# Decay rows of a bidirectional SSD scan: forward in the first 64 partitions, backward in the other 64

## The chip, the cores and the metric

One core of a Trainium2 chip. The metric is the device time of one execution in microseconds, the median of several runs. The core has a matrix engine (TensorE, PE in the profile), a vector engine (VectorE, DVE), an activation engine (ScalarE, ACT), a general engine (GpSimd, POOL) and a queue that issues the DMAs (SyncE, SP). SBUF is the on-chip memory of 128 partitions, PSUM the memory that TensorE writes.

## The reference

An inference step with two layers over 128 prompt tokens and 512 sample tokens of width 1024. Layer 0 is a Conformer convolution branch. Layer 1 is a bidirectional Mamba-2 (SSD) branch with 32 heads of 64 channels, 4 groups of 8 heads, a state of 128, and chunks of 128 tokens. All is in float32.

```
xbc = silu(depthwise_conv(xbc, w_conv, b_conv))          # 5 taps
dt_f = softplus(dtr_f + bias_f);  dt_b = softplus(dtr_b + bias_b)
# ssd_scan, once forward, once on the flipped sequence; per chunk and head:
a_cum = cumsum(dt * a_neg)
seg = a_cum[..., :, None] - a_cum[..., None, :]
decay_mat = exp(where(lower, seg, -inf))
cb = einsum('bclgn,bcsgn->bcgls', cc, bc)
y_diag = einsum('bcgrls,bcsgrp->bclgrp', cb[:, :, :, None] * decay_mat, xdt)
chunk_states = einsum('bcsgn,bcgrs,bcsgrp->bcgrpn', bc, exp(a_cum[..., -1:] - a_cum), xdt)
y_off = einsum('bclgn,bcgrpn,bcgrl->bclgrp', cc, prev_state, exp(a_cum))
...
y = y_f + flip(y_b) + d_skip * xs
y = rms_norm_per_group(y * silu(z)) * norm_g
return y @ w_out, final states
```

For a source token s and a destination l of one chunk, the forward scan contributes where s <= l and the backward scan where s >= l. The kernel holds both in one 128 x 128 matrix per head: forward decay on one side of the diagonal, backward decay on the other; the diagonal's second share is added by itself.

## The kernel before

Layer 0 fills the time up to about 590 us and isn't touched. Layer 1 (`lp` pools, from line 590 of the code on) works on 640 tokens, 128 features to a tile. A weight tile of 128 x 1024 is loaded, split into a high part (ACT, L789) and a low part (a subtraction on DVE or POOL, L793), and multiplied by the modulated input in three passes (L827): 48 matmuls of 384 or 256 columns for each of the x, B, C and z tiles. The x, B and C tiles are then convolved (one ACT and four DVE instructions, L867 and L869), transposed to tokens (L893), and used by the SSD groups. `o` items are the output projection of a finished group. The last group's output projection and the final norm end the program (L1329 and after).

Before any group can begin, `time_steps` computes the step sizes on DVE and ACT (a chain of some 30 instructions over 128 x 384), writes the cumulated rows to a DRAM tensor `acd` (rows 0 to 63 forward, 64 to 127 backward, 32 heads for either half of the chunks) and turns four results into columns by TensorE transposes (`turn_columns`, L1460 to L1465). `cols1` holds, for each chunk, per source token the column of `v` (number 0) and an exponential (number 1); `cols2` holds the two weights.

A decay matrix is made in halves of four heads (`decay_half`): `gf` (forward rows) and `gb` (backward rows), 128 x 512 each, come by DMA from `acd`, with each row repeated over all 128 partitions. POOL subtracts a column value from each (L983, once for `gf`, once for `gb`), DVE copies `gb` over `gf` where a mask says so (L984), ACT takes the exponential (L986). DVE then multiplies by the C-B products in PSUM (L1161), and TensorE multiplies with x (`py`, L1170). There are 4 groups, 5 chunks and 2 halves: 40 of them. `gf` has 4 buffers, `gb` 2.

Other POOL work: `xw` (L1034), the decay of the states (L1053), the skip term and the sum of the states' share (`y`, L1117 and L1108).

The order of layer 1's instructions on each engine is made when the program is built, by a small planner (`class Order`). Each piece of work is a generator that yields operations with an engine and an expected duration; the planner keeps one clock for each engine, and issues at each step the operation that can start first, ties broken by a priority from `PRIO`. `either` offers two engines, the second with a bias in us. Rings (`get`, `put`) model the buffers, keys (`post`, `key`) the dependences. `PLAN` is the written order of the projections: `x20` is the tile 0 of group 2, and so on. The engines then run their lists in this order and wait on semaphores.

Of the kernel before, what the change touches and what calls it, by code (L numbers as in the profile page):

```python
# [41 lines left out]
def trunk(ctx: ExitStack, tc: tile.TileContext, a: dict):  # L42
# [574 lines left out]
    if True:  # L617
# [15 lines left out]
        msk = lp.tile([P, P], I32, name="msk")  # L633
# [28 lines left out]
        PE, ACT, VE, PO, SP = range(5)  # L662

        class Order:
            def __init__(self):
                self.clock = [0.0] * 5
                self.table = None
                self.keys = {}
                self.rings = {}
                self.chains = []  # L670
                self.count = 0
# [47 lines left out]
            def run(self, until=None):  # L719
                while self.chains:  # L720
# [4 lines left out]
                    for ch in self.chains:  # L725
                        if ch[4][0] != "op":
                            continue
                        ways, bias = (*ch[4][1:], 0.0)[:2]
                        for n, (eng, dur, fn, table) in enumerate(ways):
                            wait = MARGIN[eng] if ch[5] != eng else 0.0  # L730
                            t = max(self.clock[eng], ch[1] + wait)
                            load = 1.28 if table and table != self.table else 0.0
                            key = (t + 0.4 * load if len(ways) == 1 else t + dur - ways[0][1] + bias * n, ch[2], ch[3])
                            if best is None or key < best[0]:
                                best = key, ch, eng, t + load, dur, fn, table
                    if best is None:
                        break
                    _, ch, eng, t, dur, fn, table = best
# [3 lines left out]
                    self.clock[eng] = t + dur  # L742
                    ch[1] = t + dur + LATE.get(eng, 0.0)
# [5 lines left out]
        PRIO = {"x_after": 2, "filler": 3, "decay_half": 3, "decay_state": 1, "chain0": 0, "chain1": 0, "other_y": -3, "copy_y": -1, "split_y": -1, "groups": 0, "decays": -1, "norms": -3, "gate": 3, "products1": 3, "products0": 2, "residual0": 1, "final0": -2, "w_chain": 0, "time_steps": 1, "columns": 0, "logarithm": 0, "rows_out": 0, "ends_out": 1, "weights_out": 0, "first_steps": 0, "b_after": -2, "c_after": 0, "z_after": 2, "split": 3, "add_residual": 2, "out_weights": 1, "free_bc": -1, "final1": 3, "prompt": -3, "residual1": 0, "store": -1}  # L749
# [17 lines left out]
        for name, n in (("wf", 2), ("wh", 3), ("wl", 3), ("up", 0), ("xs", 3), ("bc", 2), ("Bt", 1), ("xt", 2), ("zs", 1), ("st", 6), ("xw", 2), ("gf", 4), ("gb", 2), ("y", 1), ("y3", 0), ("yo", 2), ("yhl", 0), ("tr", 1), ("b", 3)):  # L767
            run.ring(name, n)
# [11 lines left out]
        def w_load(i, src):  # L780
# [14 lines left out]
            def split():  # L795
# [3 lines left out]
                t = yield either((VE, 1.25, lambda: low(V)), (PO, 2.45, lambda: low(G)))  # L799
# [58 lines left out]
        def convolve(ps, j, tag, bufs, name, cell, u=None):  # L858
# [9 lines left out]
            for d in range(1, 5):  # L868
                t = yield op(VE, 0.95, lambda: V.scalar_tensor_tensor(out=acc, in0=u[:, d : d + PW], scalar=c("w_c", j * 5 + d), in1=acc, op0=ALU.mult, op1=ALU.add))  # L869
# [108 lines left out]
        def decay_half(g, n, hq, gf, gb, t0):  # L978
            ch, o8 = ORDER[g][n], 8 * g
            gfh, gbh = (z_.rearrange("p (h n) -> p h n", h=4) for z_ in (gf, gb))  # L980
            for back, gt in enumerate((gfh, gbh)):
                o = 32 * back + o8 + 4 * hq
                yield op(PO, 1.15, lambda: G.tensor_sub(out=gt, in0=gt, in1=cols1[ch][:, o : o + 4].unsqueeze(2).broadcast_to([P, 4, 128])))  # L983
            t = yield op(VE, 1.1, lambda: V.copy_predicated(out=gfh, mask=msk.unsqueeze(1).broadcast_to([P, 4, 128]), data=gbh))  # L984
            put("gb", t)
            t = yield op(ACT, 0.63, lambda: S.activation(out=gfh, in_=gfh, func=AF.Exp), "exp")  # L986
            grp[g][n, hq] = gfh
            post(("gf", g, n, hq), t)

        def decays():  # L990
            yield key(("cols",))
            for g in range(NG):
                for n, ch in enumerate(ORDER[g]):
                    for hq in range(2):
                        tiles = []
                        for back, (nm, bufs) in enumerate((("gf", 4), ("gb", 2))):
                            yield get(nm)

                            def load():
                                gt = lp.tile([P, 512], F32, tag=nm, bufs=bufs, name=nm)  # L1000
                                r, col = at(back, ch, 8 * g + 4 * hq)
                                nc.sync.dma_start(out=gt.rearrange("p (h n) -> p h n", h=4), in_=acd[r : r + 4, col : col + 128].unsqueeze(0).broadcast_to([P, 4, 128]))
                                tiles.append(gt)
                            t = yield op(SP, 0.1, load)
                        start(decay_half(g, n, hq, *tiles, t), t)

        def group(g):
# [23 lines left out]
            def chunk_state(ch, back, cell, *need):  # L1031
                yield get("xw")
                xw = lp.tile([P, 512], F32, tag="xw", bufs=2, name="xw")
                t = yield op(PO, 1.12, lambda: G.tensor_mul(out=D8(xw), in0=D8(xt[ch]), in1=bc64(cols2[ch], 32 * back + o8)))  # L1034
# [9 lines left out]
            def decay_state(step, back):  # L1044
# [8 lines left out]
                t = yield op(PO, 1.15, lambda: G.tensor_mul(out=D8(new), in0=D8(sts[back, ch]), in1=dec))  # L1053
# [3 lines left out]
            def chain(back):  # L1057
                for step in range(3):
# [8 lines left out]
                    t = yield op(VE, 0.62, lambda: V.tensor_add(out=new, in0=new, in1=cell[0]))  # L1067
# [26 lines left out]
            def states_y(ch, y, n):  # L1094

                l0 = cofs(ch)
                for back in range(2):
# [8 lines left out]
                    t = yield op(VE, 0.64, lambda: V.tensor_mul(out=D8(yo), in0=D8(po), in1=bc64(cols1[ch], (64, 96)[back] + o8)))  # L1106
                    put("b", t)
                    t = yield op(PO, 1.35, lambda: G.tensor_add(out=y, in0=y, in1=yo))  # L1108
# [3 lines left out]
            def other_y(ch, co, n):  # L1112
# [4 lines left out]
                t = yield op(PO, 1.25, lambda: G.tensor_mul(out=D8(y), in0=D8(xt[ch]), in1=co.unsqueeze(2).broadcast_to([P, 8, 64])))  # L1117
# [15 lines left out]
                t = yield op(VE, 0.62, lambda: V.tensor_add(out=xt[ch], in0=xt[ch], in1=pt))  # L1133
# [10 lines left out]
            for n, ch in enumerate(order):  # L1144
# [11 lines left out]
                t = yield op(VE, 0.4, lambda: V.scalar_tensor_tensor(out=co, in0=cols2[ch][:, 96 + o8 : 104 + o8], scalar=cbd, in1=c("d", o8, 8), op0=ALU.mult, op1=ALU.add))  # L1156
                start(other_y(ch, co, n), t)
                yield key(("gf", g, n, 0), ("gf", g, n, 1))
                gfs = [grp[g][n, hq] for hq in range(2)]
                for gf in gfs:  # L1160
                    t = yield op(VE, 0.64, lambda: V.tensor_mul(out=gf, in0=gf, in1=pcb[:, 0:128].unsqueeze(1).broadcast_to([P, 4, 128])))  # L1161
# [10 lines left out]
                put("gf", t)  # L1172
# [12 lines left out]
        def gate(g, ch):  # L1185
# [5 lines left out]
            t = yield op(VE, 0.68, lambda: V.tensor_mul(out=zv, in0=zv, in1=yv))  # L1191
# [6 lines left out]
        def norm(g, sides):  # L1198
# [9 lines left out]
            for j in range(4):  # L1208
                sqs = {}
                for b in sides:  # L1210
# [4 lines left out]
                    yield either((ACT, 0.46, lambda: S.activation(out=sq, in_=zv, func=AF.Square)), (VE, 0.48, lambda: V.tensor_mul(out=sq, in0=zv, in1=zv)), bias=0.3)  # L1215
# [15 lines left out]
            yield op(VE, 1.1, lambda: V.reciprocal(out=rq, in_=rq))  # L1231
            for b in sides:
# [9 lines left out]
                for j in range(4):  # L1242
# [6 lines left out]
                    t = yield op(VE, 0.48, lambda: V.scalar_tensor_tensor(out=t_[:, sl], in0=t_[:, sl], scalar=c("sn_g", 4 * g + j), in1=ps[b][:, 0:HN], op0=ALU.mult, op1=ALU.mult))  # L1249
# [10 lines left out]
        def split_y(g, j, b, sl, t_, hi, lo):  # L1260
            yield op(ACT, 0.46, lambda: S.copy(out=hi[:, sl], in_=t_[:, sl]))
            t = yield op(VE, 0.45, lambda: V.tensor_sub(out=lo[:, sl], in0=t_[:, sl], in1=hi[:, sl].bitcast(F32)))  # L1262
# [368 lines left out]
```

## Time and profile before

| | |
|---|---|
| median of 3 runs | 1142.01 us (1140.27 to 1146.13) |
| profiled execution | 1145.75 us, span 1144.0 us |
| TensorE busy | 1076.4 us (94%), mean granted clock 0.983 |
| DVE busy | 844.4 us (74%) |
| ACT busy | 557.3 us (49%) |
| POOL busy | 580.7 us (51%) |
| DMA | 121.20 MB, 106 GB/s over the span |

Matmuls are pipelined and their ends are modelled, so TensorE's busy share says that it had work, not that it ran at its best rate. A group of instructions is shown with its count, its busy time and the mean of one; `x <- y` behind a wait says whose result ended it. In a table of stages, each engine's busy time in the stretch is followed by its number of instructions, then come the granted TensorE clock (1.00 is full), the DMA share and GB/s.

### The profile page before, as it was taken

The page shows a single profiled execution, that of the slowest core. Times are in us where ns is not written, and L with a number is a line of the kernel's source. Part 1 is how long each engine was busy: PE and PEld are TensorE (multiplying, and loading weights), DVE is VectorE, ACT ScalarE, POOL GpSimd, SP SyncE. Part 2 cuts the span into 40 slices and gives each one's busy share as a digit, 9 for nine tenths or more (in the row PEclk, how much of TensorE's full clock was granted, in tenths as well). Part 3 has the DMA queues.
Part 4 walks back from the last instruction along what each step waited for, and adds up shares of the span by engine and source line. Part 5 has one row for each costly group of instructions (what it writes and reads, how often), then busy time and mean ns, then how long its engine had stood idle before and what let it go on. Part 6 is the DMA issues. An engine that isn't in the chain of part 4 may idle for free.

```text
span 1144.0 us, 18912 instructions
## 1 busy us (share of the span) xinstructions
PE 1076.4 (94%) x7560; PEld 979.3 (86%) x7560; DVE 844.4 (74%) x1170; ACT 557.3 (49%) x873; POOL 580.7 (51%) x483
## 2 busy tenths in 40 slices
PE   6999999998999999999997999999999999999986
PEld 3898888887998998999897998898789879979875
DVE  2588999899889679413569776979776876785853
ACT  6534456456545366312465653565535552654431
POOL 1156798778778547200022166545653775466411
PEclk9999999999999999999998999999999999999997
DMA  9443324322221211613313333351444344334202
GB/s 360 155 130 129 102 85 148 129 93 92 93 75 56 74 37 38 203 56 121 101 39 88 102 120 111 105 155 37 130 111 134 106 121 120 111 102 116 60 1 92
DMA packets 79046, 121.20 MB, mean 106 GB/s; under 512 B 5488, under 2 KB 49008, under 8 KB 78960
## 3 DMA queue, kind: packets, MB, share of 16 engines
q1 hardware_dynamic: 78960, 120.01, 33.3%
q8 instruction: 59, 0.97, 0.3%
q14 instruction: 27, 0.22, 0.1%
HBM read 115.07 MB, written 4.92 MB: 105 GB/s over the span
## 4 chain that ended last, share of the span: by engine, by line
PE 70%; DVE 17%; ACT 5%; issue 3%; DMA 2%; POOL 2%; SPq 1%; DVEq 0%; POOLq 0%; ACTq 0%
PE xs L827 7%; PE pz L827 7%; PE o L827 6%; PE o L1329 3%; DVE cva L361 3%; PE po L1102 2%; PE C L827 2%; PE pst L1039 2%; DVE cn L524 2%; PE py L1170 2%; ACT wh L78 2%; DVE yhl L1262 1%; PE o__5398 L148 1%; PE o__4929 L148 1%; PE o__4927 L148 1%
## 5 line engine op out<-in xcount | busy, mean ns | idle before, releaser
L361 DVE SCALAR_TENSOR_TENSOR cva<-v,cst,cva 128x550 f32<-128x550 f32 (+12 forms) x386 | 285.9, 815 | 10.2 <-ACT cva L354 8.7
L80 POOL TENSOR_TENSOR wl<-wf,wh 128x1024 fp32r<-128x1024 f32 (+1 forms) x50 | 119.0, 2380 | 122.6 <-ACT wh L78 117.7
L78 ACT CAST wh<-wf 128x1024 fp32r<-128x1024 f32 (+1 forms) x75 | 71.4, 955 | 180.3 <-PE o__4929 L148 37.4
L390 POOL TENSOR_TENSOR cv<-cv,tp 128x490 f32<-128x490 f32 (+3 forms) x94 | 113.3, 1209 | 14.1 <-ACT cv L388 9.4
L827 PE MATMUL o<-yhl,wh 128*128 128x320 f32 x384 | 93.4, 330 | 0.0
L827 PE MATMUL pz<-h_hi,wh 128*128 128x384 f32 (+1 forms) x256 | 87.3, 341 | 2.6 <-ACT up L856 1.3
L385 ACT ACTIVATE tp<-v,cst 128x490 f32<-128x490 f32 (+3 forms) x94 | 65.7, 715 | 40.5 <-POOL cv L390 40.5
L869 DVE SCALAR_TENSOR_TENSOR xs<-up,cst,xs 128x642 f32<-128x642 f32 x64 | 74.1, 1158 | 14.4 <-ACT xs L867 13.2
L1108 POOL TENSOR_TENSOR y<-y,yo 128x512 f32<-128x512 f32 x32 | 50.8, 1588 | 65.2 <-DVE yo L1106 61.6
L827 PE MATMUL pz<-h_hi,wl 128*128 128x384 f32 (+1 forms) x256 | 79.2, 309 | 0.0
L827 PE MATMUL pz<-h_lo,wh 128*128 128x384 f32 (+1 forms) x256 | 79.0, 309 | 0.0
L80 DVE TENSOR_TENSOR wl<-wf,wh 128x512 fp32r<-128x512 f32 (+1 forms) x25 | 27.2, 1087 | 66.4 <-ACT wh L78 66.3
L827 PE MATMUL xs<-h_hi,wh 128*128 128x384 f32 (+1 forms) x224 | 76.0, 339 | 0.0
L789 ACT CAST wh<-wf 128x1024 fp32r<-128x1024 f32 x53 | 55.5, 1049 | 40.7 <-PE o L827 13.4
L827 PEld LDWEIGHTS o<-yhl,wh 128*128 128x128 f32 x384 | 65.0, 191 | 7.4 <-issue 7.4
L793 DVE TENSOR_TENSOR wl<-wf,wh 128x1024 fp32r<-128x1024 f32 x43 | 57.5, 1338 | 18.4 <-ACT wh L789 18.2
L827 PE MATMUL xs<-h_hi,wl 128*128 128x384 f32 (+1 forms) x224 | 69.3, 309 | 0.0
L827 PE MATMUL xs<-h_lo,wh 128*128 128x384 f32 (+1 forms) x224 | 69.1, 309 | 0.0
L983 POOL TENSOR_TENSOR gf<-gf,cols 128x512 f32<-128x512 f32 x40 | 50.2, 1255 | 28.0 <-DMA gf<-acd 26.3
L827 PE MATMUL o<-yhl,wl 128*128 128x320 f32 x192 | 60.0, 312 | 0.0
L628 POOL MEMSET up<- 128x2 f32 x2 | 0.2, 99 | 117.2 <-DVE h_lo L219 117.2
L983 POOL TENSOR_TENSOR gb<-gb,cols 128x512 f32<-128x512 f32 x40 | 50.0, 1250 | 12.0 <-DMA gb<-acd 11.8
(678 smaller groups left out, 3484.6 us busy)
## 6 DMA issues: line engine op xcount, KB each, us to landing
wf<-w_in SPq DMA_DIRECT2D x48, 512.0 KB, 3.6
wa<-w_ada SPq DMA_DIRECT2D x64, 256.0 KB, 4.8
wf<-w_out SPq DMA_DIRECT2D x24, 512.0 KB, 3.7
wf<-w_xbc SPq DMA_DIRECT2D x24, 512.0 KB, 3.6
gf<-acd SPq DMA_DIRECT2D x40, 256.0 KB, 4.1
gb<-acd SPq DMA_DIRECT2D x40, 256.0 KB, 4.8
wa<-w_ada SPq DMA_DIRECT2D x16, 512.0 KB, 9.9
wf<-w_z SPq DMA_DIRECT2D x16, 512.0 KB, 3.6
```

The source lines that it names most:

```text
L78: S.copy(out=wh[:, :n], in_=wf[:, :n])
L80: sub.tensor_sub(out=wl[:, :n], in0=wf[:, :n], in1=wh[:, :n].bitcast(F32))
L148: T.matmul(ps[:, b, at : at + t1 - t0], lhsT=w, rhs=h[:, t0:t1], start=first and n == 0, stop=last and n == 2)
L361: V.scalar_tensor_tensor(out=rows(acc)[:, :, lo:hi], in0=rows(v)[:, :, lo + d : hi + d], scalar=w_dw(i, tap), in1=rows(acc)[:, :, lo:hi], ...
L385: S.activation(out=tp[:, :, 0 : hi - lo], in_=rows(v)[:, :, lo + d : hi + d], func=AF.Copy, scale=w_dw(i, tap))
L390: G.tensor_add(out=rows(out)[:, :, lo:hi], in0=rows(out)[:, :, lo:hi], in1=tp[:, :, 0 : hi - lo])
L789: S.copy(out=cell["wh"], in_=cell["wf"])
L793: e_.tensor_sub(out=cell["wl"], in0=cell["wf"], in1=cell["wh"].bitcast(F32))
L827: T.matmul(ps[:, b, at_ : at_ + t1 - t0], lhsT=w_, rhs=t_[:, t0:t1], start=k == 0 and n == 0, stop=k == nk - 1 and n == 2)
L869: t = yield op(VE, 0.95, lambda: V.scalar_tensor_tensor(out=acc, in0=u[:, d : d + PW], scalar=c("w_c", j * 5 + d), in1=acc, op0=ALU.mult, ...
L983: yield op(PO, 1.15, lambda: G.tensor_sub(out=gt, in0=gt, in1=cols1[ch][:, o : o + 4].unsqueeze(2).broadcast_to([P, 4, 128])))
L1108: t = yield op(PO, 1.35, lambda: G.tensor_add(out=y, in0=y, in1=yo))
```

## The change

A decay matrix is now made per chunk, for all 8 heads of a group. `gf` is 128 x 1024: its first 64 partitions hold the forward rows, the other 64 the backward rows. Outside the two diagonal 64 x 64 blocks that is already the right direction. `gb` is 128 x 512 and holds, for the diagonal blocks alone, the other direction. The column of the base direction is no longer subtracted: it goes into the exponential as its bias (one ACT instruction per head), so its sign is turned in `time_steps`. For `gb`, POOL subtracts the difference of the two columns, which `turn_columns(0)` now computes; for this it copies its two partition halves by themselves. Two predicated copies, one for each half of the partitions, bring the diagonal blocks into `gf`. The rings shrink to 2 `gf` of double size and 2 `gb`; the last squares of side 0 use the ring `st` in place of `gf`.

The planner gets a label `VL` for DVE operations that, together with POOL's, share one more clock, `port`: neither starts before it. Durations, priorities and the order in `PLAN` are changed as well. The computation of the result is otherwise the same.

```diff
-        msk = lp.tile([P, P], I32, name="msk")
+        msk = lp.tile([P, 64], I32, name="msk")
...
-        PE, ACT, VE, PO, SP = range(5)
+        PE, ACT, VE, PO, SP, VL = range(6)
...
+                            shared = eng in (PO, VL)
+                            eng = VE if eng == VL else eng
                             wait = MARGIN[eng] if ch[5] != eng else 0.0
-                            t = max(self.clock[eng], ch[1] + wait)
+                            t = max(self.clock[eng], ch[1] + wait, self.port if shared else -99.0)
...
                     self.clock[eng] = t + dur
+                    if shared:
+                        self.port = t + dur - 0.2 * (eng == PO)
...
-        PRIO = {"x_after": 2, "filler": 3, "decay_half": 3, "decay_state": 1, ..., "time_steps": 1, ...}
+        PRIO = {"low": 2, "x_after": -1, "filler": 3, "decay_half": 0, "decay_state": -3, ..., "time_steps": 2, ...}
...
-                t = yield either((VE, 1.25, lambda: low(V)), (PO, 2.45, lambda: low(G)))
+                t = yield either((VL, 1.22, lambda: low(V)), (PO, 2.45, lambda: low(G)), bias=PRIO["low"])
...
-        def decay_half(g, n, hq, gf, gb, t0):
+        def decay(g, n, gf, gb, t0):
             ch, o8 = ORDER[g][n], 8 * g
-            gfh, gbh = (z_.rearrange("p (h n) -> p h n", h=4) for z_ in (gf, gb))
-            for back, gt in enumerate((gfh, gbh)):
-                o = 32 * back + o8 + 4 * hq
-                yield op(PO, 1.15, lambda: G.tensor_sub(out=gt, in0=gt, in1=cols1[ch][:, o : o + 4].unsqueeze(2).broadcast_to([P, 4, 128])))
-            t = yield op(VE, 1.1, lambda: V.copy_predicated(out=gfh, mask=msk.unsqueeze(1).broadcast_to([P, 4, 128]), data=gbh))
+            gv, bv = (z_.rearrange("p (h n) -> p h n", h=8) for z_ in (gf, gb))
+            yield op(PO, 1.05, lambda: G.tensor_sub(out=bv, in0=bv, in1=bc64(cols1[ch], 32 + o8)))
+            for r in (slice(0, 64), slice(64, 128)):
+                t = yield op(VL, 0.75, lambda: V.copy_predicated(out=gv[r, :, r], mask=msk[r].unsqueeze(1).broadcast_to([64, 8, 64]), data=bv[r]))
             put("gb", t)
-            t = yield op(ACT, 0.63, lambda: S.activation(out=gfh, in_=gfh, func=AF.Exp), "exp")
-            grp[g][n, hq] = gfh
-            post(("gf", g, n, hq), t)
+            grp[g][n] = gv
+            for h_ in range(8):
+                t = yield op(ACT, 0.26, lambda: S.activation(out=gv[:, h_, :], in_=gv[:, h_, :], func=AF.Exp, bias=cols1[ch][:, o8 + h_ : o8 + h_ + 1]), "exp")
+                if h_ % 4 == 3:
+                    post(("gf", g, n, h_ // 4), t)
...
+                        gf = lp.tile([P, 1024], F32, tag="gf", bufs=2, name="gf")
+                        gb = lp.tile([P, 512], F32, tag="gb", bufs=2, name="gb")
+                        for z_, n_, flip in ((gb, 64, True), (gf, 128, False)):
+                            for i in range(2):
+                                r, col = at(i != flip, ch, 8 * g)
+                                col += 64 * (flip and i)
+                                nc.sync.dma_start(out=z_[64 * i : 64 * i + 64].rearrange("p (h n) -> p h n", h=8), in_=acd[r : r + 8, col : col + n_].unsqueeze(0).broadcast_to([64, 8, n_]))
+                    t = yield op(SP, 0.3, load)
...
-        SQ = (("gf", 4), ("xs", 3))
+        SQ = (("st", 6), ("xs", 3))
...
-        PLAN = "z00 x02 b0 c0 x10 x03 z01 x11 x12 z02 b1 x20 x21 z03 x13 x30 x22 x31 c1 z10 b2 z11 x23 x32 c2 o00 ..."
+        PLAN = "x02 b0 c0 z00 x03 z01 z02 x10 c1 x20 x11 x12 z03 x13 x21 x30 b1 x22 c2 z10 z11 z12 x31 o00 ..."
...
-            yield tts(0.56, V.tensor_sub, out=v, in0=ac, in1=v)
+            yield tts(0.56, V.tensor_sub, out=v, in0=v, in1=ac)
...
+                for i in range(2):
+                    r = slice(64 * i, 64 * i + 64)
+                    for d in range(2):
+                        yield op(ACT, 0.28, lambda: S.copy(out=cv_[r, 0:3, d], in_=pv[r, :, d != i, 0, :]))
+                        yield op(VE, 0.2, lambda: V.tensor_copy(out=cv_[r, 3:5, d], in_=pv[r, 0:2, d != i, 1, :]))
+                z_ = yield op(VL, 0.3, lambda: V.tensor_sub(out=cv_[:, :, 1], in0=cv_[:, :, 0], in1=cv_[:, :, 1]))
...
-    z["msk"] = np.tril(np.ones((P, P), np.int32), -1)
+    lower = np.tril(np.ones((64, 64), np.int32), -1)
+    z["msk"] = np.concatenate([lower, 1 - lower])
```

In `time_steps` and the later vector work (convolution, gates, squares, low parts of y) the label `VE` becomes `VL` where both inputs lie in SBUF; the other changed durations are small (0.62 to 0.69 and the like).

More of the change, by code (lines that the diff above doesn't have):

```diff
@@ L993, in decays, with load @@
                 for n, ch in enumerate(ORDER[g]):
[L994 to L1005, printed above, removed]
+                    yield get("gf")
+                    yield get("gb")
+                    tiles = []
+                    def load():
+                        gf = lp.tile([P, 1024], F32, tag="gf", bufs=2, name="gf")
+                        gb = lp.tile([P, 512], F32, tag="gb", bufs=2, name="gb")
+                        tiles.extend((gf, gb))
+                        for z_, n_, flip in ((gb, 64, True), (gf, 128, False)):
[4 more added lines that the diff above has]
+                    t = yield op(SP, 0.3, load)
+                    start(decay(g, n, *tiles, t), t)
         def group(g):
@@ L1359, in item @@
             items.append((gen, src))
[L1361 removed]
+        PLAN = "x02 b0 c0 z00 x03 z01 z02 x10 c1 x20 x11 x12 z03 x13 x21 x30 b1 x22 c2 z10 z11 z12 x31 o00 o01 o02 x23 b2 z13 x32 o03 b3 x33 z20 z21 o10 z22 z23 z30 c3 o11 z31 o12 o13 z32 z33 o20 o21 o22 o23"
         for name in PLAN.split():
```

57 lines of the change are left out of this document (29 added, 28 removed).

## The prediction

> **What bounds the kernel now.** I read the page's first part, then the table of stages, since the change touches only layer 1 (from about 590 us). The table's columns are each engine's busy time in the stretch, then the granted TensorE clock and the DMA share.
>
> ```profile
> span 1144.0 us, 18912 instructions
> ...
> PE 1076.4 (94%) x7560; PEld 979.3 (86%) x7560; DVE 844.4 (74%) x1170; ACT 557.3 (49%) x873; POOL 580.7 (51%) x483
> ```
>
> ```profile
> 590.00:613.04 23.04, 19.21 (x126) 19.00 (x126) 21.52 (x24) 13.09 (x19) 9.85 (x4) 1.00 0.30 92
> 613.04:623.28 10.24, 6.05 (x27) 6.05 (x28) 9.46 (x16) 4.46 (x9) 0.32 (x1) 0.50 0.23 71
> 623.28:1022.64 399.36, 389.98 (x2661) 350.16 (x2660) 311.10 (x406) 210.89 (x334) 220.47 (x167) 1.00 0.38 111
> 1022.64:1026.05 3.41, 3.41 (x13) 3.00 (x11) 2.62 (x5) 3.11 (x5) 1.36 (x1) 0.50 0.71 208
> 1026.05:1085.00 58.95, 58.95 (x396) 50.04 (x396) 40.16 (x66) 24.03 (x35) 33.38 (x27) 1.00 0.31 90
> 1085.00:1126.00 41.00, 34.90 (x216) 29.54 (x215) 18.95 (x45) 12.10 (x25) 8.72 (x10) 1.00 0.00 1
> ```
>
> TensorE is the bound: in the 399 us of projections and SSD groups it idles 399.36 - 389.98 = 9.4 us, while POOL is at 55%. The change removes no matmul, so it can only buy back TensorE's holes. From 590 to 1085 they are 3.8 us (590 to 613), 4.2 us (613 to 623) and 9.4 us; and where the clock was 0.50, half the busy time is lost too: 6.05 / 2 = 3.0 us and 3.41 / 2 = 1.7 us. Together 22.1 us: that is the most this change can bring, short of the last stage, which it leaves alone. Next, who makes the holes: what TensorE waited for from 600 us on (us in total, times, longest).
>
> ```profile
> PE pt L1460 <- DVE v L1396: 7.1, 1, 7.1
> PE o L1329 <- DVE x L1299: 6.1, 13, 0.8
> PE pty L1129 <- POOL y L1108: 4.3, 3, 1.5
> PE po L1102 <- DVE stn L1067: 2.3, 1, 2.3
> ```
>
> The second belongs to the last products, after 1085 us. The first stands in the head: the transpose of `v` is issued to TensorE before DVE has computed `v`. Its rows, and those of the POOL work beside it (start, duration):
>
> ```profile
> 617.23 0.90 PE L1460 MATMUL pt<-cst,v 128*128 128x128 f32 x3 [7.11 <-DVE v L1396]
> ```
>
> ```profile
> 595.19 5.07 POOL L793 TENSOR_TENSOR wl<-wf,wh 128x1024 fp32r<-128x1024 f32 x2 [12.99 <-ACT wh L789]
> 602.28 2.44 POOL L793 TENSOR_TENSOR wl<-wf,wh 128x1024 fp32r<-128x1024 f32 x1 [2.02 <-ACT wh L789]
> 610.70 2.34 POOL L793 TENSOR_TENSOR wl<-wf,wh 128x1024 fp32r<-128x1024 f32 x1 [5.97 <-ACT wh L789]
> ```
>
> ```profile
> 598.04 2.64 DVE L1396 TENSOR_TENSOR t<-t 128x384 f32<-128x384 f32 x1
> 600.72 0.56 DVE L1393 SCALAR_TENSOR_TENSOR u<-t 128x384 f32<-128x384 f32 x1
> 601.31 5.61 DVE L1393 SCALAR_TENSOR_TENSOR u<-u,t 128x384 f32<-128x384 f32 x6
> ...
> 610.74 4.09 DVE L1396 TENSOR_TENSOR_SCAN rp<-one,q 64x384 f32<-64x384 f32 x2
> 614.86 1.14 DVE L1396 TENSOR_TENSOR t<-rp 64x384 f32<-64x384 f32 x2
> ```
>
> A 128x384 step takes 0.56 us alone. Beside the POOL subtraction of 595 us `t` takes 2.64 (2.1 too many), beside that of 602 the six `u` take 5.61 in place of 3.36 (2.25 too many), and beside that of 610.7 the two scans take 4.09 where the planner reckons 1.9 (2.2 too many). That is 6.5 of the 7.1 us: POOL and DVE held each other up, the planner did not know it, and put the transpose too early. The same collision through the whole layer (ns: minimum, median, maximum):
>
> ```profile
> L984 DVE COPY_PREDICATED gf<-msk,gb x40: 716/744/1873, 653.5 to 1068.6; 128x512 f32<-128x512 int32 x40
> L869 DVE SCALAR_TENSOR_TENSOR xs<-up,cst,xs x64: 784/889/2705, 592.5 to 911.6; 128x642 f32<-128x642 f32 x64
> L1108 POOL TENSOR_TENSOR y<-y,yo x32: 1266/1297/2983, 689.8 to 1076.1; 128x512 f32<-128x512 f32 x32
> L793 DVE TENSOR_TENSOR wl<-wf,wh x43: 1155/1224/2320, 589.5 to 1086.3; 128x1024 fp32r<-128x1024 f32 x43
> L1161 DVE TENSOR_TENSOR gf<-gf,pcb x40: 671/678/683, 671.1 to 1071.7; 128x512 f32<-128x512 f32 x40
> ```
>
> Operations whose inputs both lie in SBUF stretch to two or three times their median; L1161, with one input in PSUM, never does. The new planner's `VL` label marks the first kind.
>
> **The change part by part.**
>
> ```profile
> L983 POOL TENSOR_TENSOR gf<-gf,cols 128x512 f32<-128x512 f32 x40 | 50.2, 1255 | 28.0 <-DMA gf<-acd 26.3
> L983 POOL TENSOR_TENSOR gb<-gb,cols 128x512 f32<-128x512 f32 x40 | 50.0, 1250 | 12.0 <-DMA gb<-acd 11.8
> L986 ACT ACTIVATE gf<-gf x40: 614/632/656, 658.1 to 1070.4; 128x512 f32<-128x512 f32 x40
> L947 ACT ACTIVATE zs<-pz x16: 268/272/295, 598.7 to 1056.6; 128x128 f32<-128x128 f32 x16
> L1465 DVE COPY cols<-pt x4: 283/288/292, 619.4 to 638.8; 128x128 f32<-128x128 f32 x4
> gb<-acd SPq DMA_DIRECT2D x40, 256.0 KB, 4.8
> ```
>
> Subtractions on POOL: 80 of 128x512 become 20. 60 x 1.25 = 75 us leave POOL (100.2 to 25). POOL waits are only 4.3 us of TensorE's holes, so the direct worth is at most that; the larger part is that DVE meets POOL less often.
>
> Predicated copies: 40 stay 40, of 64 partitions x 512 elements. Half the partitions need not be cheaper: two 64x384 steps took 1.14 us, 0.57 each, as 128x384 does (0.56). Bounds 0.37 (if time fell with the partitions) and 0.74 us; I take 0.74, so nothing changes.
>
> Exponentials on ACT: 40 of 128x512 (25.3 us) become 160 of 128x128 with a bias. Below, the same elements at the same rate, 25.3 us; above, the 0.272 us of the 128x128 row, 43.5 us, nearest in shape: +18 us on an engine at 211 of 399 us. A chunk's exponentials then take 8 x 0.272 = 2.2 us in place of 1.26. Their cover is the next chunk's buffer: the products (L1170) are not among TensorE's waits, and two chunks' worth of `gf` still exists. If the cover were gone, 20 x 0.9 = 18 us.
>
> DMAs: 80 issues on SP stay 80, now four in a row per chunk; bytes fall from 80 x 256 KB to 20 x 768 KB. A weight load queued behind a batch starts two issues later at most; no TensorE wait is put down to a weight. `gb` now moves in pieces of 64 floats, 256 B, where all were 512 B. The trace has no such transfer; bounds are 0 and one more landing time, 4.8 us, once, at the first chunk, since later chunks are fetched ahead; I take 0.
> The Trainium skill, page "DMA: Bandwidth & Descriptors", section Specifications, speaks against this step: it wants 512 B or more per transfer for line rate. By it the first chunk would land later by up to those 4.8 us, and the sum below would be -7 in place of -12; the trace shows no load of this kind.
>
> Column transposition for `v`: one ACT and one DVE copy become four of each and a subtraction, one after the other: at the 0.288 us of the DVE copy each (ACT's taken alike, an estimate), 9 - 2 = 7 of them, 2.0 us later for the first group. TensorE then has projections queued; bounds 0 and 2.0, I take 0. The mask's smaller load and the other ring for the last squares: nothing, since both fall where no one waits.
>
> Planner (`VL`, new priorities, new item list): the head's subtractions now see the port taken by DVE's chain, so with the bias of 2 us they go to DVE (1.224 each) rather than POOL. Three of them add 3.7 us to the chain and free it of 6.5. What matters more is that planned and real end agree, so the transpose stands behind projections that are ready: the stall is a wrong place, not a lack of work. Worth between 0 and 7.1 + 3.0 (slow clock after it) = 10.1 us; the new priorities also put the convolution (2 to -1) ahead of the time steps (1 to 2), which takes some back: I take -7, nearer the full row, since the cause is named by three rows. The three waits for `y`, 4.3 us: between 0 and 4.3, I take -4, as POOL's queue ahead of them is mostly L983. The last hole:
>
> ```profile
> 1021.73 1.22 PE L1102 MATMUL po<-stn,C 128*128 128x512 f32 x2 [2.27 <-DVE stn L1067]
> 1016.00 4.47 DVE L1262 TENSOR_TENSOR yhl<-zs,yhl 128x320 fp32r<-128x320 f32 x4
> 1104.29 1.69 DVE L1262 TENSOR_TENSOR yhl<-zs,yhl 128x320 fp32r<-128x320 f32 x4
> ```
>
> Four splits took 4.47 us where the same four later took 1.69, and `stn` was late by 2.3 us. With the clock's 1.7 us this hole is worth 0 to 4.0; I take -3.
> The clock's share shows in the 0.50 of the stretch from 1022.64. The Trainium skill, page "TensorE: Matmul & The Clock Gate", Part 1, lets the clock fall only after an idle window of about 3.4 us; by that a wait of 2.27 us costs no clock, and this term would be at most 2.3. The trace differs (0.50 granted right behind the wait), and the measurement decides.
>
> New small stalls of the reordered program: as much as the smallest hole shown, 2.3 us; I take +2.
>
> Sum: -7 - 4 - 3 + 2 = -12 us. The profiled execution took 1145.75 us (span 1144.0 and 1.75 around it), 3.7 above the median of 1142.0: 1133.7 for it, 1130 for the median.
>
> **The rivals.** *Waits that only move.* The holes close and others open: DVE is on the chain of waits in the middle too.
>
> ```profile
> 716.87 1.54 DVE xs L869
> ...
> 725.71 2.96 DVE zs L1191 x2
> ```
>
> There group 0's first gates hold up TensorE, and DVE is at 311 of 399 us whatever POOL does. For it: DVE loses no instruction and gains the weight subtractions that POOL had, the head's four at least (4 x 1.224 = 4.9 us). Against it: L869 there runs 1.54 in place of 0.89, which is contention and shrinks. It gives back 8 to 12 us: 1138 to 1146, about 1142.
>
> *Slower: the time steps come late.* The first two tiles have four L869 each; with the convolution ahead, some six more of them (an estimate from the priorities; 6 x 0.889 = 5.3 us) and three subtractions (3.7) come into DVE's chain before `v`, against 6.5 saved, and the columns take 2.0 longer: the first group starts 4.5 us later. The item list asks for group 2's first tile as the 10th item, not the 12th, and needs the buffer that group 0's gates free. If these come later than TensorE gets there, it stalls for the 4.5 and for part of two items, which take about 7.1 us each (48 matmuls at 389.98 / 2661 = 0.147), and runs at half clock after. Priced at 4.5 + 7.1 + 3.0 = 14.6, less the 7 for the other holes: +8, 1150. It decides from about 8 us of lateness on; against it stand POOL's 12 fewer subtractions (15 us) before the first gate.
>
> *Everything closes.* All 22 us: 1120. It needs every wait foreseen; DVE's place on that chain speaks against it.
>
> *The change misses the port.* If the stretched rows had another cause, POOL's relief alone is left: -4, 1138, counted with the first rival.
>
> **How the numbers follow.** Forecast, 1124 to 1136: 0.52, as each term has its row. All holes closed: 0.12. Waits moved: 0.20. Late time steps: 0.16. About 0.5% (5.7 us) is what a measurement can tell from no change: faster means below 1136.3 and is 0.52 + 0.12 = 0.64; same 0.20; slower 0.16. The range reaches from 1117 (all holes and a little of the last stage) to 1149, half of the slow case. The likeliest case alone is 1124 to 1136.
>
> **What would show it.** POOL busy about 75 to 100 us lower; ACT 18 higher; medians of L869 and its like unchanged and their means nearer to them; the wait for `v` under 2 us and no stretch of clock 0.50 around 615; `pty` gone from TensorE's waits. Wrong, if TensorE waits over 5 us in one place for `cols`, `xt` or a gate, if products wait for `gf` behind ACT, or if POOL waits long for `gb`.

## The result, and the profile after

The changed kernel took 1128.96 us (median of 4 runs, 1128.39 to 1134.03) against 1144.07 for the kernel before on the same chip (1140.27 to 1146.69, 4 runs): ratio of the means 0.988, 95% interval 0.9837 to 0.9924. On another chip it was 0.9847 (0.9824 to 0.9869). The forecast was 1130, in the range 1117 to 1149, with 0.64 for faster. The size came out; two of the reasons behind it did not, or only in part, as the experiments show. Two executions on record lie far above their like (1205.73 us of the kernel before, 5394.90 of an experiment's kernel whose others took 1133 to 1140) and are left out of the ratios.

The first part of the page of the changed kernel (busy time, share of the span, instructions):

```profile
span 1126.8 us, 19050 instructions
...
PE 1067.4 (95%) x7560; PEld 974.3 (86%) x7560; DVE 835.5 (74%) x1186; ACT 579.1 (51%) x991; POOL 481.2 (43%) x413
```

The matmuls are the same 7560. POOL fell from 580.7 to 481.2 us: 60 of its subtractions went, and 10 of 128x1024 weights (483 to 413 instructions). ACT rose by 21.8. DVE fell by 8.9 though these ten weight subtractions came to it.

The stages of layer 1 after, columns as before (PE, PEld, DVE, ACT, POOL, then clock, DMA share and GB/s):

```profile
589.00:760.00 171.00, 169.04 (x1167) 156.58 (x1168) 145.70 (x186) 117.08 (x210) 46.85 (x34) 1.00 0.43 108
760.00:783.16 23.16, 19.83 (x144) 17.30 (x142) 16.67 (x30) 13.88 (x27) 11.41 (x10) 1.00 0.45 117
783.16:789.99 6.83, 2.87 (x9) 2.88 (x10) 4.17 (x4) 1.43 (x4) 2.69 (x3) 0.50 0.33 100
789.99:1066.00 276.01, 276.01 (x1873) 243.27 (x1872) 209.39 (x311) 145.73 (x279) 104.87 (x82) 1.00 0.35 93
1066.00:1108.00 42.00, 37.74 (x241) 33.81 (x240) 19.12 (x46) 11.28 (x23) 8.74 (x10) 1.00 0.05 16
1108.00:1126.80 18.80, 9.35 (x54) 8.76 (x52) 8.49 (x21) 1.47 (x4) 0.00 (x0) 0.58 0.39 139
```

What TensorE waited for from 600 us on (us in total, times, longest):

```profile
PE pz L832 <- ACT zs L952: 7.2, 1, 7.2
PE o L1339 <- DVE x L1309: 4.2, 8, 0.8
PE pst L1050 <- POOL xw L1045: 0.8, 1, 0.8
```

The waits for `v`, `y` and `stn` are gone. The head has no hole (1.96 us idle in 171), and after 790 there is none for 276 us. One new hole of 7.2 us has opened, which ends at 787, with the clock at 0.50 for 6.83 us from within it on. Against the stages before: the stretch up to the last products took 495 us (590 to 1085) and takes 477 (589 to 1066). TensorE's idle time in it went from 17.4 to 2.0 + 3.3 + 4.0 = 9.3 us, the loss to half clock from 4.7 to 2.87 / 2 = 1.4. That is 11.4 of the 18 us. The other 6.6 are in part no gain at all, for the two stretches do not hold the same work (rows of before, then of after):

```profile
590.00:1085.00 495.00, 477.61 (x3219) 428.26 (x3220) 384.86 (x514) 255.59 (x400) 265.38 (x198) 0.99 0.36 108
1085.00:1144.00 59.00, 43.44 (x263) 37.49 (x261) 27.31 (x65) 13.09 (x28) 8.72 (x10) 0.87 0.13 45
```

```profile
589.00:1066.00 477.00, 467.75 (x3189) 420.03 (x3190) 375.93 (x529) 278.12 (x519) 165.82 (x128) 0.99 0.38 100
1066.00:1126.80 60.80, 47.09 (x293) 42.56 (x291) 27.61 (x66) 12.74 (x27) 8.74 (x10) 0.87 0.16 54
```

Thirty matmuls have moved into the last stage, about 4.4 us at 477.61 / 3219 = 0.148 each (an estimate). They stand there among the last products, and so the last stage takes only 1.8 us more (59.0 to 60.8) with thirty matmuls more: TensorE's idle time in it fell from 15.6 to 13.7, and its waits for `x` from 6.1 to 4.2. Layer 1 as a whole is 16.2 us shorter: 11.4 from the holes and the clock up to the last products, 1.9 from the waits of the last stage, and some 3 in which TensorE counts as busy, which stay open and are no more than executions of one kernel differ by. It also starts 1 us earlier, behind a layer that the change does not touch: 17.2 us in the span, where the medians are 15.1 apart.

The rows that answer to the collision rows of before (ns: minimum, median, maximum):

```profile
L990 DVE COPY_PREDICATED gf<-msk,gb x40: 718/747/1833, 665.4 to 1044.9; 64x512 f32<-64x512 int32 x40
L874 DVE SCALAR_TENSOR_TENSOR xs<-up,cst,xs x64: 873/888/1802, 592.9 to 910.7; 128x642 f32<-128x642 f32 x64
L994 ACT ACTIVATE gf<-gf,cols x160: 384/388/406, 671.7 to 1050.5; 128x128 f32<-128x128 f32 x160
```

```profile
L874 DVE SCALAR_TENSOR_TENSOR xs<-up,cst,xs 128x642 f32<-128x642 f32 x64 | 62.8, 982 | 9.4 <-ACT xs L872 8.2
L994 ACT ACTIVATE gf<-gf,cols 128x128 f32<-128x128 f32 x160 | 50.0, 390 | 11.8 <-DVE gf L990 11.6
```

The medians on DVE are those of before, 889 and 744, within 3 ns. The longest convolution step fell from 2705 to 1802 ns, and the mean from 1158 to 982. The collision has become rarer, not gone.

The new hole, on four engines (start, duration; in brackets the idle time before, and what ended it):

```profile
778.69 1.68 DVE L1272 TENSOR_TENSOR yhl<-zs,yhl 128x320 fp32r<-128x320 f32 x4
780.30 1.27 DVE L1078 TENSOR_TENSOR stn<-stn,pst 128x512 f32<-128x512 f32 x2
781.50 4.71 DVE L1272 TENSOR_TENSOR yhl<-zs,yhl 128x320 fp32r<-128x320 f32 x4
```

```profile
782.07 1.29 POOL L1045 TENSOR_TENSOR xw<-xt,cols 128x512 f32<-128x512 f32 x1
783.32 1.28 POOL L988 TENSOR_TENSOR gb<-gb,cols 128x512 f32<-128x512 f32 x1
784.57 1.28 POOL L1045 TENSOR_TENSOR xw<-xt,cols 128x512 f32<-128x512 f32 x1
```

```profile
786.30 0.60 ACT L951 ACTIVATE zs<-pz 128x512 f32<-128x512 f32 x1 [8.36 <-DVE yhl L1272]
```

```profile
787.12 0.69 PE L832 MATMUL pz<-h_hi,wh 128*128 128x384 f32 x1 [7.20 <-ACT zs L952]
```

Four splits take 1.68 us with POOL out of the way, and 4.71 beside three POOL operations: `zs` is freed 3 us late. That is less than half of the wait of 7.2 us; for the rest, `pz` stood in TensorE's list before its buffer could come free. A wait of the kind that the change closed elsewhere has opened here.

### The profile page after: what moved, and what is told of

Its sections match the earlier page's. It is cut to its first block, busy times and chain, and to the rows that moved or that the text cites. A ratio compares the mean times of both kernels' runs of the same rounds, so it can differ in the third digit from the quotient of the medians.

```text
span 1126.8 us, 19050 instructions
## 1 busy us (share of the span) xinstructions
PE 1067.4 (95%) x7560; PEld 974.3 (86%) x7560; DVE 835.5 (74%) x1186; ACT 579.1 (51%) x991; POOL 481.2 (43%) x413
## 4 chain that ended last, share of the span: by engine, by line
PE 78%; DVE 9%; ACT 5%; DMA 4%; issue 3%; SPq 1%; POOL 1%; DVEq 0%; ACTq 0%
PE pz L832 10%; PE xs L832 8%; PE o L832 8%; PE o L1339 3%; DVE cva L361 3%; PE B L832 3%; PE po L1113 2%; PE pst L1050 2%; PE C L832 2%; DVE cn L524 2%; PE py L1181 2%; ACT wh L78 2%; PE o__5398 L148 1%; PE o__5399 L148 1%; PE o__4929 L148 1%
## 5 line engine op out<-in xcount | busy, mean ns | idle before, releaser
L798 DVE TENSOR_TENSOR wl<-wf,wh 128x1024 fp32r<-128x1024 f32 x53 | 70.9, 1338 | 11.0 <-ACT wh L794 9.2
L874 DVE SCALAR_TENSOR_TENSOR xs<-up,cst,xs 128x642 f32<-128x642 f32 x64 | 62.8, 982 | 9.4 <-ACT xs L872 8.2
L832 PEld LDWEIGHTS pz<-h_hi,wh 128*128 128x128 f32 x256 | 48.9, 191 | 12.2 <-ACT zs L952 7.4
L1064 POOL TENSOR_TENSOR stn<-st_f,decb 128x512 f32<-128x512 f32 x4 | 5.1, 1273 | 125.3 <-DMA gb<-acd 74.4
L994 ACT ACTIVATE gf<-gf,cols 128x128 f32<-128x128 f32 x160 | 50.0, 390 | 11.8 <-DVE gf L990 11.6
```

What stands on the lines that cost most here:

```text
L798: e_.tensor_sub(out=cell["wl"], in0=cell["wf"], in1=cell["wh"].bitcast(F32))
L832: T.matmul(ps[:, b, at_ : at_ + t1 - t0], lhsT=w_, rhs=t_[:, t0:t1], start=k == 0 and n == 0, stop=k == nk - 1 and n == 2)
L874: t = yield op(VL, 0.89, lambda: V.scalar_tensor_tensor(out=acc, in0=u[:, d : d + PW], scalar=c("w_c", j * 5 + d), in1=acc, op0=ALU.mult, ...
L994: t = yield op(ACT, 0.26, lambda: S.activation(out=gv[:, h_, :], in_=gv[:, h_, :], func=AF.Exp, bias=cols1[ch][:, o8 + h_ : o8 + h_ + 1]), ...
```

## The experiments

Ratios are to the kernel before, measured beside it on the same chip, with the 95% interval. Its median was 1144 to 1148 us on the chips used, so the ratios are compared and not the times. "Full" is the changed kernel. A diff is against full, unless it says otherwise, and shows only the lines that matter.

**The change in two halves.** First, the new decay structure alone, in the old order (in words: + what it has of the change, - what it leaves out):

```diff
+ decay(), gf 128 x 1024, bias in the exponential, four DMAs per chunk
- VL, the port clock, new durations, priorities and PLAN
+ "decay": 3      # as decay_half had
```

> The new decay matrix alone (per chunk, one subtraction, bias in the exponential, new column transposition), with the planner, durations, priorities and item list of before. Theory A (the gain is TensorE's holes that DVE and POOL collisions make, and both parts are needed: the decay takes 75 us off POOL, the planner closes the hole of 7.1 us in the head): the head's hole and its slow clock stay (11 us), the waits for y (4.3) and the late stn (4.0) shrink; 1136 to 1140 us where before has 1144 and the full change 1129. Rival B (the lighter POOL is all of it): 1129 to 1131, head hole gone or paid for. Rival C (the new order is all of it): 1144.

1.0014 (0.9999 to 1.003). What TensorE waited for in it:

```profile
PE pt L1465 <- DVE v L1401: 7.1, 1, 7.1
...
PE xs L827 <- DVE x L958: 2.9, 1, 2.9
...
PE pty L1135 <- POOL y L1114: 0.8, 2, 0.5
```

POOL's relief does what was said of it: the waits for `y` shrink from 4.3 to 0.8 us. But projections now wait for DVE's update of `x` (2.9 and 1.6 us), the head keeps its hole, and nothing is gained.

Second, the new planner with the old decay (in words again):

```diff
+ VL, the port clock, new durations, priorities and PLAN
+ "decay_half": 1
- decay(); decay_half() stays, its operations with the new labels
```

> The planner's part alone: shared port, new durations, priorities and item list, with the old decay matrix in halves (80 POOL subtractions of 1.04 us). Theory A: the head's hole closes (-9 to -11), POOL's 80 subtractions still collide with DVE in the middle and the port is 62 us fuller, so new or old holes of 3 to 6 us remain there: 1134 to 1139. Rival B: 1144 or more. Rival C: 1129.

1.0123 (1.0096 to 1.0149), slower; Theory A expected a gain, and only Rival B's "1144 or more" has room for it. The waits:

```profile
PE pz L832 <- ACT zs L952: 7.1, 1, 7.1
PE o L832 <- DVE x L963: 6.6, 1, 6.6
...
PE py L1175 <- ACT gf L991: 5.1, 1, 5.1
PE pz L832 <- ACT up L861: 3.8, 1, 3.8
```

None of these is in the head, where the longest wait is 1.3 us. The new order has four long waits where POOL still does the 80 subtractions. So the halves are worth about 0 and +1.2%, and together about -1.4%: the effects do not add.

**The port clock.** Full, with the planner unaware of the port:

```diff
-                            shared = eng in (PO, VL)
+                            shared = False
```

> The full change, but the planner's shared clock is switched off, so that VL counts as VE; durations, priorities and item list stay. Theory A: weight subtractions go to POOL again while DVE runs the time steps, some planned ends come too early; 3 to 12 us are lost, 1132 to 1141, with a wait of TensorE over 2 us in the head. Rival C (priorities and list alone): 1129.

0.9916 (0.9896 to 0.9936). Against the 0.988 and 0.9847 of full, the port clock is worth 4 to 8 us; the intervals overlap with the first of the two and not with the second. The expected wait in the head did not come: without the port the head has no TensorE wait over 1.3 us either, though a weight subtraction went to POOL there and eight convolution steps beside it took 9.26 us in place of 7.22. The loss is spread over many small waits, the longest 2.2 us.

**POOL's load put back.** Three more subtractions of zero on `gb` per chunk, planned, in the chain that leads to the exponential:

```diff
...
+            for _ in range(3):
+                yield op(PO, 1.05, lambda: G.tensor_sub(out=bv, in0=bv, in1=bc64(zero, 0)))
```

> The full change with three more POOL subtractions (of zero, on gb) per chunk, planned with their duration: POOL has its 80 subtractions back, all else is the new form. Theory A, part 1 (POOL's load is worth what its collisions cost, though it is planned): +3 to +8 us, 1132 to 1137; the means of DVE's two-SBUF-input operations rise. Rival: what is planned is hidden, 1129.

1.0101 (1.008 to 1.0123), some 25 to 30 us slower than full; both expectations were lower. Its longest TensorE waits are 7.1 us for `up`, 6.6 for `y` and 3.8 for `xw`. Nearly the same load beside the chain, four subtractions per chunk on a tile of their own that nothing waits for:

```diff
+            start(aside(), t)
...
+            for _ in range(4):
+                yield op(PO, 0.87, more)       # G.tensor_sub(out=idle, in0=idle, in1=idle), 128 x 320
```

> The full change with four extra POOL subtractions of 128x320 on a tile of their own per chunk (80 x 0.87 us), planned, at the lowest priority, off every chain: nothing waits for them but what is behind them on POOL and what meets them at SBUF. Theory A (POOL's load costs by collisions with DVE and by its place in the order): 5 to 25 us slower than the full change. Rival (E4's 30 us were the longer chain of its decay): within 4 us of the full change.

And with memsets of about the same duration in their place, in the same order on every engine:

```diff
-            G.tensor_sub(out=idle, in0=idle, in1=idle)
+            G.memset(idle, 0.0), G.memset(idle, 0.0), G.memset(idle[:, 0:128], 0.0)
```

> As the kernel with the four extra subtractions, in the same order on every engine, but with memsets of about the same duration, which write SBUF and read nothing. Theory A (it is two inputs from SBUF on DVE against POOL's reads): DVE's stretched operations return to the means of the full change, and it is 3 to 12 us faster than the one with subtractions. Rival (POOL's time or the planner's order, not the collision): the two agree within 2 us.

0.9903 (0.9881 to 0.9925) and 0.988 (0.9862 to 0.9899); full, measured beside them:

> The full change once more, beside the three that follow, on their chip: 0.988 of before, as first measured.

0.9847 (0.9824 to 0.9869). Layer 1 of the subtracting and of the memset kernel in one row each, then one line of DVE in both:

```profile
589.00:1132.00 543.00, 516.67 (x3480) 460.25 (x3480) 415.63 (x591) 290.21 (x549) 249.66 (x218) 0.98 0.34 94
```

```profile
589.00:1130.00 541.00, 515.02 (x3480) 459.90 (x3480) 396.44 (x591) 290.65 (x549) 248.59 (x378) 0.99 0.34 94
```

```profile
L1211 DVE TENSOR_TENSOR zs<-zs,xt 128x512 f32<-128x512 f32 x20 | 17.9, 933 | 0.1
```

```profile
L1211 DVE TENSOR_TENSOR zs<-zs,xt 128x512 f32<-128x512 f32 x20 | 13.9, 734 | 0.1
```

POOL is equally busy (249.7 and 248.6 us) and DVE does the same 591 instructions, but takes 19.2 us longer beside POOL operations that read SBUF. This shows the collision itself. The Trainium skill, page "SBUF — State Buffer", section "SBUF: two separate sides", says that a DVE operation with two SBUF inputs contends only with a GpSimd operation that reads SBUF; the trace agrees (415.63 against 396.44 us). Yet the 19 us of DVE cost the kernel little: the medians are 1136.04 us and 1132.84, and the two intervals overlap, so the 3.2 us between them are not clear of noise. Against full (1128.83 us) the subtracting kernel is 7.2 us slower, in another order, one without full's wait of 7.2 us; the price of the load alone is not divided from that of the order. The same kind of load in the decay chain cost about four times as much. That was a different order too, so lateness in the chain and a worse order are not divided either.

**The order alone.** Full with the priorities and the item list of before:

```diff
- PRIO = {"low": 2, "x_after": -1, ..., "time_steps": 2, ...};  PLAN = "x02 b0 c0 z00 x03 ..."
+ PRIO = {"x_after": 2, "decay": 3, "low": 2, ..., "time_steps": 1, ...};  PLAN = "z00 x02 b0 c0 x10 ..."
```

> The full change with the priorities and the item list of before: new decay matrix, shared port clock and new durations stay. Theory A as the earlier runs leave it (the port clock is worth some 7 us, the decay alone nothing, and the rest is a list that fits the new decay's times): head hole closed, but waits of the middle opened as in the run of the decay alone, 1136 to 1146. Rival (the port clock finds a good order from any list): 1127 to 1133.

0.9979 (0.9965 to 0.9993). Port clock, new labels and decay are all there, and 2 us of gain are left. TensorE's first wait:

```profile
PE xs L832 <- DVE wl L798: 8.7, 2, 7.9
```

The 7.9 us wait is in the head again and ends at 605.57: the weight subtraction that the port moved from POOL to DVE now stands behind the time steps, and TensorE starves for it. Next, full with the old item list alone:

```diff
- PLAN = "x02 b0 c0 z00 x03 z01 z02 x10 ..."
+ PLAN = "z00 x02 b0 c0 x10 x03 z01 x11 ..."
```

> The full change with the item list of before alone; the new priorities stay (convolution ahead of the time steps). Theory (the head is closed by the priorities, the list only fits the middle): no wait of TensorE over 2 us before 640 us, holes in the middle, 1132 to 1141. Rival (list and priorities work only together): 1143 or more, as with both old.

0.9893 (0.9866 to 0.9919), with no head wait over 1.3 us. So the priorities carry most of the order's worth, and the list some 2 to 5 us of it. Last, full with two priorities alone put back, so that the time steps go ahead of the convolution of x:

```diff
- "x_after": -1, ... "time_steps": 2
+ "x_after": 2, ... "time_steps": 1
```

> The full change with two priorities of before: time steps 1, convolution 2, so that DVE's time steps go ahead of the first convolutions and the columns come about 15 us earlier. The prediction's step (the new priorities take back some of the gain in the head, since the columns come late): 0 to 4 us faster than the full change. Rival (late columns cost nothing, since TensorE has projections, and early time steps hold up the convolutions that free its buffers): 3 to 20 us slower, with TensorE waits for up or xs.

1.0022 (1.0009 to 1.0035), slower: all of the gain is lost. Its waits, and the rows of the two shown:

```profile
PE pt L1470 <- DVE v L1406: 9.5, 1, 9.5
...
PE C L832 <- ACT up L861: 1.4, 1, 1.4
```

```profile
613.10 0.87 PE L1470 MATMUL pt<-cst,v 128*128 128x128 f32 x3 [9.51 <-DVE v L1406]
616.62 0.69 PE L832 MATMUL C<-h_hi,wh 128*128 128x384 f32 x1 [1.45 <-ACT up L861]
```

The wait for `v` is back and longer, and right behind it TensorE waits for the copy of a finished projection into `up`, the buffer of the convolution: only this copy frees the room in PSUM that C needs. The clock is at 0.50 for 13.65 us, from within the first wait on. In this head the scans of DVE ran undisturbed (1.93 us for the two), POOL did nothing, and the planner knew the port. So a head without the collision, and with a planner that sees it, still has its hole when the time steps go first; without the port but with the new priorities it has none. The order decides. (In the kernel before, the collision did make `v` late, by the 6.5 us that the prediction reads; no run takes it out of that very order.)

**The exponentials.** Full with one exponential of 128 x 1024 in place of eight, in the same order; the bias is left out:

```diff
-                t = yield op(ACT, 0.26, lambda: S.activation(out=gv[:, h_, :], ..., bias=cols1[ch][...]), "exp")
+                t = yield op(ACT, 0.26, lambda: h_ or S.activation(out=gv, in_=gv, func=AF.Exp), "exp")
```

> The full change in the same order, but the eight exponentials with bias of a chunk are one of 128x1024 without bias, at the place of the first (the bias is left out, so y and its layer's output are of other values). ACT is freed of some 25 us in all and of 1.5 to 2 us per chunk. The prediction's step (ACT's surplus is hidden): within 3 us of the full change. Rival (ACT's 8 small instructions lie on the path from the decay to the products): 5 to 15 us faster.

0.9841 (0.9823 to 0.9859), as full (0.9847), with ACT at 551.5 us in place of 579.1. The exponentials' surplus is hidden.

**One item moved.** The hole at 787 is a `z1` item waiting for a buffer, so group 3's `x31` goes ahead of these items:

```diff
- ... x22 c2 z10 z11 z12 x31 o00 ...
+ ... x22 c2 x31 z10 z11 z12 o00 ...
```

> The full change with one item moved: x31 stands ahead of z10 z11 z12 in the item list, not behind them. In the full change TensorE waits 7.2 us at 787 us for ACT's evacuation of z, which waits for DVE's last splits of the group before (4.7 us where four take 1.7), and the clock is halved for 6.8 us. Theory: that hole is an order that came 7 us too early; with a projection of 7 us ahead of it, it closes with its slow clock: 5 to 9 us less than the full change. Rival (waits only move): the time stays within 3 us, with a new wait over 4 us.

1120.41 us (1119.24 to 1123.23), 0.9773 (0.9754 to 0.9791): faster than both kernels, 8.4 us under full (1128.83) on the same chip. Its waits and the middle of layer 1:

```profile
PE o L1339 <- DVE x L1309: 4.2, 8, 0.8
...
PE po L1113 <- DVE stn L1078: 0.3, 1, 0.3
```

```profile
760.00:1058.00 298.00, 297.73 (x2026) 262.52 (x2025) 231.04 (x344) 163.12 (x312) 117.54 (x94) 1.00 0.36 98
```

TensorE is idle for 0.27 us in 298, at full clock. The 7.2 us of wait and 1.4 of clock that the hole cost in full, 8.6, are the 8.4 us, near enough.

## Why the prediction came out, step by step

- *The head, -7.* It gave 9.1 us (11.0 of holes and clock before, 1.96 us idle now). The size held, the cause only in part. The claim that "the stall is a wrong place, not a lack of work", made right because "planned and real end agree", failed, and so did the remark that the new priorities take some back. The priorities are what closes the hole: with the two of before the kernel took 1147.99 us and had a wait for `v` of 9.5 us, with the port clock in place; with the new ones and no port clock the hole stayed closed. `v` comes 13 us later than before (629.54 against 616.6):

```profile
592.86 7.22 DVE L874 SCALAR_TENSOR_TENSOR xs<-up,cst,xs 128x642 f32<-128x642 f32 x8
...
617.80 3.53 DVE L1403 SCALAR_TENSOR_TENSOR u<-u,t 128x384 f32<-128x384 f32 x6
...
625.81 1.94 DVE L1406 TENSOR_TENSOR_SCAN rp<-one,q 64x384 f32<-64x384 f32 x2
...
629.54 0.56 DVE L1406 TENSOR_TENSOR v<-v,rp 128x384 f32<-128x384 f32 x1
```

  The six `u` and the scans are free of POOL, as forecast (3.53 and 1.94 against 5.61 and 4.09), but ahead of them DVE now does sixteen convolution steps, the first eight in a row. They free the buffers that the next projections need. In the kernel before, 18 matmuls of B stood ready behind the transpose, about 2 us at their spacing of 0.12 us; C, the next tile, needed the room in PSUM that the copy of an x tile into `up` frees, and this copy waited for a convolution that DVE did behind the time steps:

```profile
617.78 0.56 PE L827 MATMUL B<-h_hi,wh 128*128 128x256 f32 x1
```

```profile
618.93 0.75 ACT L856 COPY up<-xs 128x128 f32<-128x128 f32 x2 [0.44 <-DVE xs L869]
```

  So of the 7.1 us some 2 were a wrong place (an estimate from the 18 matmuls), and the rest was a lack of work.
- *The waits for `y`, -4.* They closed, and did so with the decay alone (0.8 us left). But in the old order other waits opened and nothing was gained (1.0014): the step took a hole's length for its worth.
- *The hole at `stn`, -3.* Gone. No run took it alone.
- *New stalls, +2.* Mis-sized: one stall of 7.2 us and 1.4 of clock, 8.6 us. The bound was taken from the smallest hole shown, where the 7.1 us in the head showed that one wait can cost one item's time. Moving the item gave 8.4 us back. A TensorE wait over 5 us in one place was also among the signs of being wrong, there for `cols`, `xt` or a gate; this one is for the buffer of the gates' input.
- *The sum, -12.* The terms for the holes and the new stalls came to 11.4 us, but by luck: more holes closed than was reckoned (all but 2.1 of the 22.1 us, where 14 were taken), and the new stall took 8.6 back, where 2 were taken.
- *Beyond the sum.* The last stage, which the prediction holds that the change "leaves alone", gave 1.9 us, since thirty matmuls filled its waits. Some 3 us more lie in stretches in which TensorE counts as busy, which the prediction held to be out of reach ("it can only buy back TensorE's holes"); what they are stays open. With the earlier start of 1 us these make the 17.2 us of the two profiled spans.
- *Parts at nothing.* The exponentials take 390 ns each where 272 was the upper bound. They overlap, and ACT is busy with them for 50.0 us, 25 more than before, where 18 was the most; still hidden, as the run with one exponential shows. The predicated copies are 747 ns at half the partitions, the price taken. The 256-B pieces delay nothing that shows: `gb` lands in 4.5 us.

```profile
gf<-acd SPq DMA_DIRECT2D x40, 256.0 KB, 4.7
...
gb<-acd SPq DMA_DIRECT2D x40, 128.0 KB, 4.5
```

- *The rivals.* "Waits that only move" is what each half of the change does by itself, and in part the whole (the hole at 787). "The time steps come late" was right in that they come late and wrong in that someone waits: the first group's own start is later (first subtraction for a decay matrix at 657.31 us, before at 638.84: 18 us, where 4.5 were reckoned), and TensorE has projections meanwhile. "Everything closes", 1120, is the time that the moved item reached, though part of it comes from beyond the holes.

The chain of work that ended last now runs less over DVE (TensorE 70% and DVE 17% before):

```profile
PE 78%; DVE 9%; ACT 5%; DMA 4%; issue 3%; SPq 1%; POOL 1%; DVEq 0%; ACTq 0%
```

This share is no measure of the gain: the kernel with the new planner alone, slower than before, has 77% and 10%.

## What to carry to other kernels

In a kernel whose engines run fixed orders, the worth of a lighter part and of a new order do not add: here 0% and +1.2% alone made about -1.4% together, so price a change with the order that goes with it, and try an order again after every change of load. A wait for a late result has two cures, to make the result earlier or to have other work ready: ask which buffers that other work needs, and who frees them. And look at the one largest wait that is left: moving one item past it was worth 8.4 us, where the whole change had given 18.8 on the same chip.

## What the runs showed of the hardware that was not expected

- An exponential of 128 x 128 with a bias column takes 384 to 406 ns, where the activation of the same shape without one, from PSUM (L947 before), took 272. The Trainium skill, page "ScalarE: Activation LUTs", section "What ACT_TABLE_LOAD costs", has this: about 280 ns + 0.833 per element with a pointer bias; for 128 elements that is an estimate of 387, which the trace's 388 agrees with. The nearest row in shape was not the nearest in operands.
- COPY_PREDICATED takes 747 ns for 64 partitions and 744 for 128, with 512 elements in each.
- 128 KB in pieces of 256 B land in 4.5 us, 256 KB in pieces of 512 B in 4.7 (`gb` before: 4.8): half the bytes saved little time. The Trainium skill, page "DMA: Bandwidth & Descriptors", section Specifications, wants 512 B or more per transfer for line rate; whether the small pieces or a fixed part of the landing time is the reason here, no run shows, and nothing waited for it.
- DVE takes 19 us more beside POOL operations that read SBUF than beside memsets of the same length, and the kernel loses at most a few of them: 3.2 us between the medians, not clear of noise.
